# A fused hybrid decoder layer on one core: the beginning reordered, the turned x kept through DRAM, bias rows copied per head pair, GpSimd ordered by hand

## The chip, the cores and the metric

The kernel runs on one core of one Trainium2 chip. The metric is the device time of one execution in microseconds (us). The kernel before takes 1002.67 us, the median of 3 runs (1002.58 to 1002.92).

## What is computed

One step of one decoder layer in float32, for a prompt of 512 tokens and, beside it, 8 samples of 4 tokens (32 more), D = 1024:

```python
def _layer(x, ...):                       # cut to what matters
    h = _rmsnorm(x, norm_mix_pre)
    xr, q, k, v, g = split(h @ w_in)      # 1024 -> 4608 columns
    lru_out = _rg_lru(_causal_dwconv(xr)) # gates, then a scan over time
    attn = _band_attention(q, k, v)       # window 128, 8 query heads on 2 kv heads, table of relative biases
    m = (sigmoid(g_lru) * (lru_out @ w_lru_o) + sigmoid(g_attn) * (attn @ w_attn_o)) @ w_out
    x = x + _rmsnorm(m, norm_mix_post)
    u = _causal_dwconv(_rmsnorm(x, norm_ffn_pre) @ w_up)          # 8192 columns, width 3
    return x + _rmsnorm((gelu(gate(u)) * val(u)) @ w_down, norm_ffn_post)
```

The last rows of the states (LRU, convolutions, keys, values) are outputs too.

## The kernel before

**Products.** Activations stand transposed in SBUF: 128 features on the partitions, 544 tokens in a row, 8 such tiles for D. Every float32 operand is split into a high and a low part of the type fp32r, so a product is three matmuls for each tile of 128: high weight by high h (`hH` with `wh`), high weight by low h (`hL`, `wh`), low weight by high h (`hH`, `wl`). A weight column block ("key") is loaded as 512 KB into one of 5 `raw` buffers; ScalarE (ACT) makes `wh` by a copy (L277), VectorE (DVE) makes `wl` by a subtraction (L282), half a key at a time. The tokens go in two halves: a = 0 is the first 256, a = 1 the other 288 (272 and 272 after the attention).

**Order.** TensorE (PE) is ordered by hand over the whole program, ACT and DVE inside the mixer (everything up to the output of `w_out`); GpSimd (POOL) and the DMA queue of SyncE (SP) are ordered by the framework's scheduler. An engine executes its own instructions in that order. `step` issues one product (24 matmuls) and then calls `tick`, which issues in this order: the `wh` splits of later weights, the side jobs that are due at this tick (generators started by `start_at`), the work on the previous product's result, the `wl` splits, and what the side jobs left in `last`. So a product's result is worked on beside the next product.

**Beginning (L357 to L463).** x0 and x1 (the first 256 tokens) come as two half rows each, are squared and summed by ACT and DVE (`xsquares`), the reciprocal root is made in six small steps (`xrstd`), x is scaled by it (`xscale`, L423 on ACT and L425 on DVE), PE turns 128x128 tiles into PSUM (`ps_ta`, L448), and `hsplit` (L431) makes `hH` on ACT and `hL` on DVE. 18 matmuls on constants keep PE busy before that. Then the first product of the first key is issued in three runs of 8 matmuls. `norm_b` (L451) does the same for the other 288 tokens between the next products (`ps_tb`, L461); its squares stand in the first tick, its root and scaling in the second, its transposes behind the third product.

**Bias table.** `attn_tables` (L544) makes 8 rows of 384 biases by a matmul, stores them in DRAM (`rscr`), and copies each 128 times in DRAM (`rrep`, one DMA of 1024 rows); `load_btab` (L577) loads for each pair of heads a skewed window of it.

**x again (L995 to L1011).** The residual needs x transposed but not normalised. While the products with `w_lru_o` (`pmlo`) run, `x_again` loads x from the inputs once more into `raw` buffers (`xx`), PE transposes it (`pxx`, L1004, 40 transposes), and ACT and DVE copy the pieces into `x1`. Beside each of these products DVE multiplies its result by the gate (L171, `gl`), POOL adds the attention's share (L1019, `gl<-gl,ga`), and ACT and DVE split the sum (`mH`, `mL`) for the product with `w_out`.

**End.** `load` (L1285) brings the weights of the second part of the layer; the last blocks of `w_up` go through `raw` buffers and are combined on DVE, `needs` (L1274) names which of them a sum needs.

## Time and profile before

| what | value |
|---|---|
| median of 3 runs | 1002.67 us |
| the profiled execution | 1003.73 us |
| its span in the trace | 1002.0 us |
| mean granted clock of TensorE | 0.997 |
| busy: PE, DVE, ACT, POOL | 988.9, 732.0, 579.4, 151.0 us |

The profiled execution is 1.73 us longer than its span (what lies ahead of the first and behind the last instruction) and 1.06 us above the median. Rows of the timeline and of the chain begin with the start and the duration in us; a row "x8" joins eight like instructions. In square brackets stands how long the engine was idle ahead of it and what released it.

### The profile page before, as it was taken

How to read it: one execution, taken by the hardware profiler on the slowest of the kernel's cores; microseconds unless marked ns; L12 is line 12 of the kernel's file. 1: busy time of each engine (PE TensorE's matmuls, PEld its weight loads, DVE VectorE, ACT ScalarE, POOL GpSimd, SP SyncE). 2: the span in 40 equal slices, each digit the busy share in tenths (PEclk: the TensorE clock that was granted, in tenths of full speed). 3: DMA queues.
4: the chain of work that ended last, by engine and by line, in shares of the span. 5: the costliest groups of instructions: out<-in, count | busy, mean ns of one | idle time of the engine just before them, and what ended most of it. 6: DMA issues, size and time to landing. Idle time of an engine off the chain costs nothing.

```text
span 1002.0 us, 20195 instructions
## 1 busy us (share of the span) xinstructions
PE 988.9 (99%) x7837; PEld 978.5 (98%) x7837; DVE 732.0 (73%) x1555; ACT 579.4 (58%) x1422; POOL 151.0 (15%) x270
## 2 busy tenths in 40 slices
PE   8999999999999999999999999999999999999997
PEld 7999999999999999999999999999999999999996
DVE  6476687545846555589777788888888888887865
ACT  6444455469358535456776756565656565656652
POOL 3131010002304432110001111111111111110004
PEclk9999999999999999999999999999999999999999
DMA  7743223333322345327245858586867676767712
GB/s 211 231 150 93 64 77 105 99 91 94 102 68 85 106 138 148 105 66 210 71 116 124 193 124 192 125 191 127 189 133 184 139 177 145 171 160 167 216 45 90
DMA packets 207687, 133.40 MB, mean 133 GB/s; under 512 B 6546, under 2 KB 194306, under 8 KB 207560
## 3 DMA queue, kind: packets, MB, share of 16 engines
q1 hardware_dynamic: 197944, 112.20, 39.4%
q0 software_dynamic: 9600, 17.90, 11.3%
q10 hardware_dynamic: 48, 2.03, 0.5%
q8 instruction: 61, 1.00, 0.4%
q14 instruction: 34, 0.28, 0.1%
HBM read 111.82 MB, written 9.14 MB: 121 GB/s over the span
## 4 chain that ended last, share of the span: by engine, by line
PE 92%; DVE 3%; ACT 2%; DMA 2%; issue 0%; SPq 0%; ACTq 0%; DVEq 0%
PE pmin L165 22%; PE pmdn L165 16%; PE pux L1400 15%; PE puy L1400 7%; PE pq L1400 6%; PE pmout L165 5%; PE pmao L165 5%; PE pmlo L165 4%; PE puz L1400 4%; PE pg L165 1%; PE psc L165 1%; PE pvp L165 1%; DMA raw_up_s<-in_w_up_dram 1%; DMA raw_in<-in_w_in_dram 1%; PE pt L701 1%; PE ptok L165 1%
## 5 line engine op out<-in xcount | busy, mean ns | idle before, releaser
L165 PE MATMUL pmin<-hH,wh_in 128*128 128x256 f32 (+1 forms) x576 | 167.8, 294 | 0.0
L165 PE MATMUL pmin<-hH,wl_in 128*128 128x256 f32 (+1 forms) x576 | 164.7, 288 | 0.0
L165 PE MATMUL pmin<-hL,wh_in 128*128 128x256 f32 (+1 forms) x576 | 164.6, 288 | 0.0
L165 PE MATMUL pmdn<-fH,wh_dn 128*128 128x256 f32 (+1 forms) x448 | 129.2, 288 | 0.2 <-DVE ft L174 0.2
L165 PE MATMUL pmdn<-fH,wl_dn 128*128 128x256 f32 (+1 forms) x448 | 129.2, 288 | 0.2 <-DVE wl_dn L168 0.2
L165 PE MATMUL pmdn<-fL,wh_dn 128*128 128x256 f32 (+1 forms) x448 | 129.1, 288 | 0.0
L177 DVE SCALAR_TENSOR_TENSOR uc<-u,fv,uc 128x560 f32<-128x560 f32 x128 | 102.0, 797 | 13.3 <-ACT uc L1431 13.2
L165 PEld LDWEIGHTS pmin<-hH,wh_in 128*128 128x128 f32 x576 | 108.9, 190 | 1.9 <-issue 1.2
L165 PEld LDWEIGHTS pmin<-hL,wh_in 128*128 128x128 f32 x576 | 108.1, 188 | 0.0
L165 PEld LDWEIGHTS pmin<-hH,wl_in 128*128 128x128 f32 x576 | 107.9, 188 | 0.0
L165 PEld LDWEIGHTS pmdn<-fH,wh_dn 128*128 128x128 f32 x448 | 84.5, 189 | 0.6 <-issue 0.6
L165 PEld LDWEIGHTS pmdn<-fH,wl_dn 128*128 128x128 f32 x448 | 84.4, 188 | 0.4 <-DVE wl_dn L168 0.4
L165 PEld LDWEIGHTS pmdn<-fL,wh_dn 128*128 128x128 f32 x448 | 84.3, 188 | 0.0
L1526 ACT COPY u<-pux 128x272 f32<-128x272 f32 x52 | 20.1, 387 | 86.1 <-PE pux L1400 86.1
L168 DVE TENSOR_TENSOR u<-puy,u 128x240 f32<-128x240 f32 (+2 forms) x78 | 24.6, 344 | 49.8 <-PE puy L1400 32.1
L174 DVE TENSOR_TENSOR ft<-ft,pmdn 128x256 f32<-128x256 f32 (+1 forms) x104 | 45.2, 436 | 16.7 <-PE pmdn L165 16.1
L277 ACT ACTIVATE wh_in<-raw_in 128x512 fp32r<-128x512 f32 x72 | 44.2, 629 | 19.3 <-PE pmin L165 8.4
L282 DVE TENSOR_TENSOR wl_in<-raw_in,wh_in 128x512 fp32r<-128x512 f32 x72 | 48.2, 683 | 0.8 <-ACT wh_in L277 0.8
L1431 ACT ACTIVATE uc<-u,fv 128x560 f32<-128x560 f32 x64 | 48.2, 754 | 0.0
L664 ACT ACTIVATE s<-s,st 128x256 f32<-128x256 f32 (+1 forms) x32 | 15.2, 475 | 50.4 <-DVE st L661 43.0
L168 DVE TENSOR_TENSOR wl_dn<-raw_dn,wh_dn 128x512 fp32r<-128x512 f32 x56 | 38.3, 684 | 0.0
L1326 POOL DMA_DIRECT2D raw_up_s<-raw_up_s x26 | 22.7, 874 | 102.9 <-issue 5.2
(776 smaller groups left out, 3404.3 us busy)
## 6 DMA issues: line engine op xcount, KB each, us to landing
raw_in<-in_w_in_dram SPq DMA_DIRECT2D x36, 512.0 KB
raw_dn<-in_w_down_dram SPq DMA_DIRECT2D x56, 256.0 KB
raw_up_s<-in_w_up_dram SPq DMA_DIRECT2D x26, 512.0 KB
raw_up_s<-raw_up_s POOLq DMA_DIRECT2D x26, 256.0 KB, 5.9
raw_ao<-in_w_attn_o_dram SPq DMA_DIRECT2D x8, 512.0 KB
raw_lo<-in_w_lru_o_dram SPq DMA_DIRECT2D x8, 512.0 KB
raw_out<-in_w_out_dram SPq DMA_DIRECT2D x8, 512.0 KB
x1d<-x SPq DMA_DIRECT2D x8, 272.0 KB
```

The source lines that it names most:

```text
L165: pe.matmul(out, l, r, start=start, stop=stop)
L168: dve.tensor_tensor(out=out, in0=a, in1=b, op=ALU.subtract)
L174: dve.tensor_tensor(out=out, in0=a, in1=b, op=ALU.add)
L177: dve.scalar_tensor_tensor(out=out, in0=a, scalar=s_, in1=b, op0=op0, op1=op1)
L277: act.activation(hl[0], raw, AF.Copy)
L282: (eng or dve).tensor_tensor(out=hl[1], in0=raw, in1=f32(hl[0]), op=ALU.subtract)
L664: act.activation(s3[:, j, :], s3[:, j, :], AF.Exp, bias=ng[:, j:j + 1], accum_out=sm[:, j:j + 1])
L701: pe.transpose(pt[:, (2 * ch + j) * P:(2 * ch + j + 1) * P], s3[:, j, ch * P:(ch + 1) * P], ident)
L1326: pool.dma_start(out=w["p4"], in_=w["p2"], accum_op=ALU.add)
L1400: pe.matmul(ps[:, :HN], w, x, start=start and k == 0 and i == 0, stop=stop and k == 3 and i == 2, skip_group_check=True)
L1431: act.activation(yt[j][:, 0:FLATU], u[:, 0:FLATU], AF.Copy, scale=fv[:, j:j + 1])
L1526: act.copy(e[nm_], z)
```

## The change

It has five parts.

1. **Beginning.** The load of the norm's weight rows goes ahead of x1 on SP; four more small loads go from POOL's queue to SP, ahead of the loads of keys 3 and 4. 12 warm matmuls stand ahead of the transpose of these rows and 11 behind it. The scaling of x0 and x1 is three halves on DVE, one on ACT, ahead of the first split of weights. The 16 transposes go into four whole PSUM banks, 8 at a time, and the splits take tiles from alternating banks. The matmuls of the first product (`first_ps`) stand between the splits: `hH` by `wh` and, one tile behind, `hL` by `wh`; the eight `hH` by `wl` come last. The `wl` of the first key is made by POOL instead of DVE. The copy of the weight rows goes from DVE to ACT.
2. **x again.** The turned, scaled x (still without the norm's weight) is copied from PSUM to SBUF: 8 copies of 128x256 and 8 of 128x288, half on ACT and half on DVE, in the first ticks (`keep_a`, `keep_b`). POOL stores the eight tiles to DRAM at ticks 13 to 20, SP stores the reciprocal of the scale. In the stage of `w_lru_o`, SP loads both back and POOL multiplies, 8 times 128x544 (L1048 of the changed kernel). The second load of x, its 40 transposes and 40 copies are gone.
3. **Bias rows.** `rrep` is four tensors of 256 rows, each written by a DMA of its own shortly before it is read.
4. **POOL by hand.** Its order inside the mixer is the program's; loads for the sample tables go from POOL's to SP's queue.
5. **End.** The last block of `w_up` comes in two halves into `s` slots (53 instead of 52) and earlier, not into a `raw` buffer.

```diff
-S_BUFS = 52
+S_BUFS = 53
...
 SAMPLE = (41, 46)
-WARM = 18
+WARM = 12
+KEEP = 11
...
     cp = mixer.enter_context(tc.tile_pool(name="mixer_const", bufs=1))
-    mixer.enter_context(tc.manual_schedule(engines={act.engine, dve.engine}))
+    mixer.enter_context(tc.manual_schedule(engines={act.engine, dve.engine, pool.engine}))
...
         n = X.half[a][1] - X.half[a][0]
-        if key == order[0] and a == 0:
-            for j, (i0, i1) in enumerate(((0, 0), (1, 0), (0, 1))):
-                for k in ks:
-                    mm(ps[:, :n], wunits[2 * wpos[key] + k // 4][i0][:, k % 4, :], X.get(k, a, i1),
-                       j == 0 and k == 0, j == 2 and k == KD - 1)
-            return
...
-        ps = PM("pm" + "_".join(str(z) for z in key) + f"_{a}")
-        if quick:
+        first_ = key == order[0] and a == 0
+        ps = first_ps if first_ else PM("pm" + "_".join(str(z) for z in key) + f"_{a}")
+        if first_:
+            pass
+        elif quick:
...
     xload(0)
+    nc.sync.dma_start(out=rows_a[0:8, :], in_=I["norm_mix_pre"].rearrange("o (k p) -> (o k) p", p=P))
     xload(1)
-    nc.sync.dma_start(out=rows_a[0:8, :], in_=I["norm_mix_pre"].rearrange("o (k p) -> (o k) p", p=P))
...
     xload(4)
-    for i in (2, 3, 4):
-        wload(i)
+    wload(2)
...
     pool.memset(relx, 1.0)
-    pool.dma_start(out=relx[0:NBK, :], in_=I["rel_bias"])
+    nc.sync.dma_start(out=relx[0:NBK, :], in_=I["rel_bias"])
     ohp = T("ohp")[:NBK + 1, 0:3 * WIN]
-    pool.dma_start(out=ohp, in_=I["c_ohp"])
+    nc.sync.dma_start(out=ohp, in_=I["c_ohp"])
     for r, nme in ((8, "norm_mix_post"), (16, "norm_ffn_pre"), (24, "norm_ffn_post")):
-        pool.dma_start(out=rows_a[r:r + 8, :], in_=I[nme].rearrange("o (k p) -> (o k) p", p=P))
+        nc.sync.dma_start(out=rows_a[r:r + 8, :], in_=I[nme].rearrange("o (k p) -> (o k) p", p=P))
+    wload(3)
+    wload(4)
...
     pe.transpose(ps0[:, 0:8], rows_a[0:8, :], ident[0:8, 0:8])
+    for z in range(KEEP):
+        mm(pw[:, (z % 4) * P:(z % 4 + 1) * P], ones, ident, True, True)
...
     xsquares(1)
+    act.copy(pv[:, 0:8], ps0[:, 0:8])
     xrstd(0, 2)
-    split = [wsplit_hi(u) for u in wclaim(2)]
-    xscale(0, "av")
-    xscale(1, "vv")
-    dve.tensor_copy(pv[:, 0:8], ps0[:, 0:8])
-    for u in split:
-        wsplit_lo(*u)
+    u0, u1 = wclaim(2)
+    def scale0(i, z):
+        dve.tensor_scalar(xt[i, z][:, 0:512], xt[i, z][:, 0:512], ss[:, 1, i:i + 1], None, ALU.mult)
+    scale0(0, 0)
+    scale0(1, 0)
+    act.activation(xt[1, 1][:, 0:512], xt[1, 1][:, 0:512], AF.Copy, scale=ss[:, 1, 1:2])
+    scale0(0, 1)
+    first_ps = PM("pm_first")
+    def first_mm(k, i0, i1, start=False, stop=False):
+        mm(first_ps[:, :256], wunits[k // 4][i0][:, k % 4, :], h.get(k, 0, i1), start, stop)
+    ps_ta = []
+    wsplit_lo(*wsplit_hi(u0), eng=pool)
+    seq = (0, 2, 1, 3, 4, 6, 5, 7)
+    for z, k in enumerate(seq + (None,) * 3):
+        if z % 4 == 0 and z < KD:
+            for kk in (z // 2, z // 2 + 1):
+                ps_ta.append(PX(f"ps_ta{kk}"))
+                for q in range(4):
+                    pe.transpose(ps_ta[-1][:, q * P:(q + 1) * P], xtile(q % 2, 2 * kk + q // 2), ident)
+        if k is not None:
+            hsplit(k, 0, ps_ta[k // 2][:, k % 2 * 256:k % 2 * 256 + 256])
+        if z == 1:
+            wsplit_lo(*wsplit_hi(u1), eng=pool)
+        if 2 <= z < KD + 2:
+            first_mm(seq[z - 2], 0, 0, start=z == 2)
+        if z >= 3:
+            first_mm(seq[z - 3], 0, 1)
     for k in range(KD):
-        ps = (PM if k in (5, 6) else PX)(f"ps_ta{k}")
-        for i in range(2):
-            pe.transpose(ps[:, i * P:(i + 1) * P], xtile(i, k), ident)
-        hsplit(k, 0, ps[:, :256])
+        first_mm(k, 1, 0, stop=k == KD - 1)
+    xn = [S(f"xn{k}") for k in range(KD)]
+    xdram = drp.tile([KD, P, NT], F32, name="xdram")
+    rms = cp.tile([P, 5], F32, name="rms")
+    rmsd = drp.tile([5, P], F32, name="rmsd")
+    def keep_a(k):
+        (dve.tensor_copy if k % 2 else act.copy)(xn[k][:, 0:256], ps_ta[k // 2][:, k % 2 * 256:k % 2 * 256 + 256])
+    def keep_b(k, ps):
+        (act.copy if k % 2 else dve.tensor_copy)(xn[k][:, 256:NT], ps[:, :288])
+    def put_away():
+        dve.reciprocal(rms, ss[:, 1, :])
+        nc.sync.dma_start(out=rmsd.rearrange("i p -> p i"), in_=rms)
+        for k in range(KD):
+            pool.dma_start(out=xdram[k], in_=xn[k][:, 0:NT])
+            yield
...
         last.extend(lambda i=i: xsquares(i) for i in (2, 3, 4))
-        yield
+        last.extend(lambda k=k: keep_a(k) for k in range(4))
+        yield
+        last.extend(lambda k=k: keep_a(k) for k in range(4, KD))
...
                 pe.transpose(ps[:, t0 - 256:t0 - 256 + n], xtile(i, k), ident[:n, :n])
-            late.append(lambda k=k, ps=ps: hsplit(k, 1, ps[:, :288]))
+            late.append(lambda k=k, ps=ps: (hsplit(k, 1, ps[:, :288]), keep_b(k, ps)))
...
     for t in range(DT):
-        pool.dma_start(out=rel4[32 * t:32 * t + 32, :], in_=I["rel_bias"])
+        nc.sync.dma_start(out=rel4[32 * t:32 * t + 32, :], in_=I["rel_bias"])
...
     rscr = drp.tile([NH, 3 * WIN], F32, name="rscr")
-    rrep = drp.tile([NH, P, 3 * WIN], F32, name="rrep")
+    rrep = [drp.tile([2, P, 3 * WIN], F32, name=f"rrep{hp}") for hp in range(4)]
...
-        a = rscr[:, :]
-        pool.dma_start(out=rrep, in_=bass.AP(a.tensor, a.offset, [[3 * WIN, NH], [0, P], [1, 3 * WIN]]))
...
         ohs = T("ohs")[:, 0:SKEY]
-        pool.dma_start(out=ohs, in_=I["c_ohs"])
+        nc.sync.dma_start(out=ohs, in_=I["c_ohs"])
...
             m_ = T(f"mk{g}")[:, 0:SKEY]
-            pool.dma_start(out=m_, in_=I["c_msk"][g])
+            nc.sync.dma_start(out=m_, in_=I["c_msk"][g])
...
+    def load_rep(hp):
+        r = rscr[2 * hp:2 * hp + 2, :]
+        pool.dma_start(out=rrep[hp], in_=bass.AP(r.tensor, r.offset, [[3 * WIN, 2], [0, P], [1, 3 * WIN]]))
...
         bt = S(f"btab{hp}")[:, 0:512].rearrange("p (h j) -> p h j", h=2)
-        src = rrep[2 * hp:2 * hp + 2, :, :]
+        src = rrep[hp][:, :, :]
...
     start_at(1, norm_b())
+    start_at(13, put_away())
...
     for hp in range(4):
-        start_at((5, 11, 18, 27)[hp], once(load_btab, hp))
+        start_at((4, 6, 13, 20)[hp], once(load_rep, hp))
+        start_at((5, 10, 17, 26)[hp], once(load_btab, hp))
...
-    def x_again(i):
-        t0, n, src = TOK[i]
-        x_i = RAW(f"xx{i}")
-        nc.sync.dma_start(out=x_i[:n, :], in_=src)
-        yield 2 + i // 4
-        for kk in range(2):
-            px = PX(f"pxx{i}_{kk}")
-            for j in range(4):
-                k = 4 * kk + j
-                pe.transpose(px[:, j * P:j * P + n], x_i[:n, k * P:(k + 1) * P], ident[:n, :n])
+    def x_again():
+        full = T("rms_full")[:, 0:NT]
+        a = rmsd[:, :]
+        nc.sync.dma_start(out=full, in_=bass.AP(a.tensor, a.offset, [[0, P], [1, NT]]))
+        for k in range(KD):
+            nc.sync.dma_start(out=x1[k][:, 0:NT], in_=xdram[k])
+        yield 3
+        for k in range(KD):
+            pool.tensor_tensor(out=x1[k][:, 0:NT], in0=x1[k][:, 0:NT], in1=full, op=ALU.mult)
             yield
-            for j in range(4):
-                k = 4 * kk + j
-                (dve.tensor_copy if j % 2 else act.copy)(x1[k][:, t0:t0 + n], px[:, j * P:j * P + n])
-    for i in range(5):
-        start_at(now[0] + 3 + 2 * i, x_again(i))
+    start_at(now[0] + 3, x_again())
...
         _, p_, nm = key
+        if p_ == 31 and nm == "a12":
+            return [("up", p_, ""), ("up", 32 + p_, ""), ("up", p_, "s")]
...
             src = w_dn[q * CH * P:(q + 1) * CH * P, c * P:(c + 1) * P]
+        elif key == ("up", 31, "s"):
+            raws[key] = [S(f"{nm}{z}")[:, 0:512].rearrange("p (k n) -> p k n", k=4) for z in range(2)]
+            for z, raw in enumerate(raws[key]):
+                nc.sync.dma_start(out=raw, in_=w_up[512 * z:512 * z + 512, 31 * P:32 * P].rearrange("(k p) n -> p k n", p=P))
+            return
...
         r = raws["up", 32 + p_ if nm in ("p1", "a22") else p_, "s" if nm in ("p2", "p4") else ""]
+        if isinstance(r, list):
+            return r[nm == "p4"]
```

Two places of the order matter for what follows. First VectorE in the beginning, from the split of the second key (`raw_in_111`) to the root for the other 288 tokens (the rows on `ss` that end with 128x3); `jv` are the squares, `kL` the work on the first product's result. Before:

```order
L282 TENSOR_TENSOR wl_in_318<-raw_in_111,wh_in_317 128x512
L282 TENSOR_TENSOR wl_in_321<-raw_in_111,wh_in_320 128x512
L409 SCALAR_TENSOR_TENSOR jv_326,ss<-x_1_115 128x512
L409 SCALAR_TENSOR_TENSOR jv_330,ss<-x_1_119 128x512
L409 SCALAR_TENSOR_TENSOR jv_334,ss<-x_1_123 32x512
L168 TENSOR_TENSOR kL_371<-pmin_0_292,kH_370 128x256
L282 TENSOR_TENSOR wl_in_363<-raw_in_125,wh_in_362 128x512
L282 TENSOR_TENSOR wl_in_366<-raw_in_125,wh_in_365 128x512
L174 TENSOR_TENSOR ss<-ss 128x3
```

The same place in the changed kernel:

```order
L408 SCALAR_TENSOR_TENSOR jv_349,ss<-x_1_123 32x512
L479 COPY xn_274<-ps_ta_209 128x256
L479 COPY xn_276<-ps_ta_214 128x256
L169 TENSOR_TENSOR kL_390<-pm_first,kH_389 128x256
L283 TENSOR_TENSOR wl_in_382<-raw_in_125,wh_in_381 128x512
L283 TENSOR_TENSOR wl_in_385<-raw_in_125,wh_in_384 128x512
L479 COPY xn_278<-ps_ta_234 128x256
L479 COPY xn_280<-ps_ta_239 128x256
L175 TENSOR_TENSOR ss<-ss 128x3
```

Four copies of the kept x now stand ahead of the root, two of them ahead of `kL` and of the split of the third key; ACT has four as well, two ahead of its split of the third key and two ahead of its square root.

Second GpSimd in the stage of `w_lru_o`; `gl` are the additions behind the products, the four DMAs store outputs of the recurrent branch. Before:

```order
L1019 TENSOR_TENSOR gl_4158<-gl_4158,ga_2728 128x272 x2
L1019 TENSOR_TENSOR gl_4247<-gl_4247,ga_2826 128x272 x2
L907 DMA out_dram<-lru_rows 3x1024
L908 DMA out_dram<-lru_rows 24x1024
L909 DMA out_dram<-lru_rows 16x1x64
L910 DMA out_dram<-lru_rows 8x1024
L1019 TENSOR_TENSOR gl_4325<-gl_4325,ga_2922 128x272 x2
```

The same place in the changed kernel, where `x_0` to `x_7` are the eight tiles of x:

```order
L1048 TENSOR_TENSOR x_3_4618<-x_3_4618,rms_full 128x544
L1059 TENSOR_TENSOR gl_4291<-gl_4291,ga_2870 128x272
L950 DMA out_dram<-lru_rows 3x1024
L951 DMA out_dram<-lru_rows 24x1024
L952 DMA out_dram<-lru_rows 16x1x64
L953 DMA out_dram<-lru_rows 8x1024
L1048 TENSOR_TENSOR x_4_4619<-x_4_4619,rms_full 128x544
L1059 TENSOR_TENSOR gl_4369<-gl_4369,ga_2966 128x272
```

A multiplication of 128x544 now stands ahead of eight of the sixteen additions, one of them behind the four DMAs as well.

## The prediction

> **What bounds the kernel now.** I read the page first: the busy times and the chain that ended last.
>
> ```profile
> PE 988.9 (99%) x7837; PEld 978.5 (98%) x7837; DVE 732.0 (73%) x1555; ACT 579.4 (58%) x1422; POOL 151.0 (15%) x270
> PE 92%; DVE 3%; ACT 2%; DMA 2%; issue 0%; SPq 0%; ACTq 0%; DVEq 0%
> ```
>
> TensorE (PE) is busy for 988.9 of 1002.0 us, and 92% of the chain is its work. So the time falls only where PE has less to do or waits less, and it rises where another engine makes PE wait. The sum of all PE idle time is 13.1 us, an upper bound for anything that only removes waits. Next I read PE's waits:
>
> ```profile
> PE ps_ta L448 <- ACT x L423: 3.4, 1, 3.4
> PE ps_warm L165 <- POOL relx L374: 1.5, 1, 1.5
> PE pxx L1004 <- DMA xx<-in_x_prompt_dram: 0.9, 1, 0.9
> ```
>
> Three waits make up nearly half of it. Two lie in the beginning, one is at the second load of x, which the change removes.
>
> **x kept through DRAM: PE loses its transposes.** The chain through the stage of `w_lru_o` shows them one group of four at a time, and the tile's own view gives the count:
>
> ```profile
> 350.67 0.44 PE pxx L1004 x4
> 368.50 4.50 DMA xx<-in_x_prompt_dram
> 373.00 0.14 issue
> 373.14 0.63 PE pxx L1004 x4
> 377.21 6.03 PE pmlo L165 x48
> 386.82 0.36 PE pxx L1004 x4
> L1004 PE MATMUL pxx<-ident,xx x40: 221/272/299, 350.5 to 387.0; 128*128 128x128 f32 x32, 32*128 32x32 f32 x8
> ```
>
> Forty transposes in ten groups: seven of 0.44 us, one of 0.63 (behind the wait), two of 0.36 for the 32 samples, in all 3.08 + 0.63 + 0.72 = 4.43 us. The products around them take 3.0 us each (6.03 for two, 24 matmuls of 0.125 us apiece) and follow without a gap, so PE's time falls by all of this. Ahead of the seventh group PE idles for 0.9 us on the load and 0.14 us on its issue, 1.0 us. This wait goes with its transposes. What is late next? The load waited for a `raw` buffer; the new loads go into `s` slots, and nothing on PE reads them here. Term: **-5.4 us**.
>
> **What is added beside it.** POOL gets eight multiplications of 128x544. The rows before have none of this shape; nearest are its two-input operations of 128x568, and DVE's scan beside one of them and without one:
>
> ```profile
> 317.94 1.76 POOL L881 TENSOR_TENSOR xc<-xc,lt 128x568 f32<-128x568 f32 x1
> 319.91 1.40 POOL L881 TENSOR_TENSOR xc<-xc,lt 128x568 f32<-128x568 f32 x1
> 326.74 1.95 POOL L881 TENSOR_TENSOR xc<-xc,lt 128x568 f32<-128x568 f32 x1 [0.68 <-ACT lt L880]
> 320.00 2.50 DVE L887 TENSOR_TENSOR_SCAN hs<-rg,xc 128x568 f32<-128x568 f32 x1 [1.58 <-POOL xc L884]
> 323.97 1.33 DVE L887 TENSOR_TENSOR_SCAN hs<-rg,xc 128x568 f32<-128x568 f32 x1
> L1019 POOL TENSOR_TENSOR gl<-gl,ga 128x272 f32<-128x272 f32 x15 | 16.3, 1087 | 35.9 <-DVE gl L171 26.1 <-ACT wh_lo L277 6.3 <-ACT wh_out L277 3.5
> 368.46 0.78 POOL L1019 TENSOR_TENSOR gl<-gl,ga 128x272 f32<-128x272 f32 x1
> 375.76 0.68 DVE L282 TENSOR_TENSOR wl_lo<-raw_lo,wh_lo 128x512 fp32r<-128x512 f32 x1
> 350.50:364.90 14.40, 14.40 (x120) 14.32 (x119) 8.49 (x21) 5.76 (x16) 3.91 (x4) 1.00 0.35 110
> ```
>
> I take 1.4 to 1.95 us for a multiplication and 1.09 for an addition, 2.5 to 3.04 a product, against the 3.0 that a product lasts: POOL, idle for 35.9 us at these additions now, becomes just about full. Behind a late addition stand ACT's `mH`, then DVE's `mL`, then the next gate multiplication and the next `wl` split, in that order. The cover is what PE has in hand: the last `wl` of the stage is done at 376.44, and its product is the second of the two that begin at 377.21; its second half, which reads this split, is reached at 377.21 + 3.02 + 1.5 = 381.7, 5.3 us later. Once the four output DMAs, which end where the addition at 368.46 begins, push POOL back by some 2 us, and a multiplication stands behind them; 2 us plus eight times 0.04 stay inside 5.3. DVE has room: 8.49 of 14.4 us, and its own copies of x go (as ACT's do). I cost this at nothing; without the cover it is the slower rival below.
>
> The Trainium skill says in "SBUF — State Buffer", section "SBUF: two separate sides", that VectorE operations with two SBUF inputs and a GpSimd operation exclude each other, the later one standing still for the whole of the other; this speaks against the change. The scan of 2.50 us agrees: 1.17 us longer than its twin, beside 1.31 us of a POOL operation. By that rule DVE could lose up to eight times 1.95 us here, and the sum would still stand while the loss stays inside the cover.
>
> **The beginning.** I put PE, ACT and DVE side by side:
>
> ```profile
> 11.07 2.90 PE L448 MATMUL ps_ta<-ident,x 128*128 128x128 f32 x16 [3.43 <-ACT x L423]
> 16.37 1.11 PE L165 MATMUL pmin<-hL,wh_in 128*128 128x256 f32 x8
> 17.32 0.28 PE L165 MATMUL pmin<-hH,wh_in 128*128 128x256 f32 x1
> 20.25 0.81 PE L165 MATMUL ps_ohp<-ohp,relx 33*8 33x384 f32 x2
> 23.92 2.19 PE L461 MATMUL ps_tb<-ident,x 128*128 128x128 f32 x12
> 9.26 1.15 ACT L277 ACTIVATE wh_in<-raw_in 128x512 fp32r<-128x512 f32 x2 [0.69 <-DMA raw_in<-in_w_in_dram]
> 10.31 0.71 ACT L423 ACTIVATE x<-x,ss 128x512 f32<-128x512 f32 x1
> 11.55 3.03 ACT L433 ACTIVATE hH<-ps_ta,pv 128x256 fp32r<-128x256 f32 x8 [0.53 <-PE ps_ta L448]
> 18.34 0.36 ACT L599 ACTIVATE kH<-pmin 128x256 fp32r<-128x256 f32 x1
> 21.66 1.34 ACT L423 ACTIVATE x<-x,ss 128x512 f32<-128x512 f32 x2 [0.83 <-DVE ss L177]
> 12.05 3.23 DVE L177 SCALAR_TENSOR_TENSOR hL<-ps_ta,pv,hH 128x256 fp32r<-128x256 f32 x8
> 18.73 0.42 DVE L168 TENSOR_TENSOR kL<-pmin,kH 128x256 fp32r<-128x256 f32 x1 [0.43 <-ACT kH L599]
> 20.27 0.16 DVE L174 TENSOR_TENSOR ss<-ss 128x3 f32<-128x3 f32 x1
> 21.66 1.67 DVE L425 TENSOR_SCALAR x<-x,ss 128x512 f32<-128x512 f32 x4
> ```
>
> Now: scaling ends at 11.02, the first `hH` starts at 11.55, the last `hL` ends at 15.28, and the two last runs of the first product go on to 17.32. In the change the scaling on ACT stands ahead of the weights (0.71 us from 9.39, since the root is ready when DVE starts its scaling), one split of 0.57 follows, and the first transposes need only the first half of the rows: `hH` can start at about 10.75. Its eight take 3.03 again, with the second split of weights between them: the last `hL` ends near 14.9. By then two of the three runs are done, and only eight matmuls remain (1.11 us, as the run at 16.37). The second product starts at about 16.0, not 17.32: PE is **1.3 us ahead**.
>
> Does it keep that? It needs x2 to x4 scaled for `ps_tb`. PE reaches these transposes after two products and the bias matmul, 23.92 - 17.32 = 6.6 us after its start: at 22.6, or about 23.0, since the split of the third key is later too (below). Now the first three halves that it needs are ready at 23.0: ACT's two end at 21.66 + 1.34, DVE's third at about the same time. So 0.9 us of slack stand before 23.92. The change puts four copies of 128x256 on each engine ahead of the root. Nearest rows: 0.36 for `kH`, 0.42 for `kL`, and 0.38 to 0.40 apiece in the rows of eight (3.03/8, 3.23/8); four are 1.4 to 1.6 us. Off this go 0.3 us, as `hL` ends earlier, and what DVE idles now ahead of `kL` (0.43) is mostly lost again, since ACT's `kH` is also two copies later. The root moves from 20.27 to about 21.5, the scaled halves from 23.0 to about 24.25, and `ps_tb` starts there instead of at 23.92. Term: **+0.3 us**, bounded by -0.9 (PE finds x ready at 23.0) and +1.2 (copies at 0.42 each on both engines, and the small loads put ahead of keys 3 and 4 delay a weight by some tenths). PE's lead of 1.3 us is then spent waiting. The 11 added matmuls lie in the 3.43 us wait and cost nothing.
>
> **The end.** The last block of `w_up` is on the chain, and PE waits there a little:
>
> ```profile
> 917.04 7.29 DMA raw_up_s<-in_w_up_dram
> 928.31 0.28 PE L165 MATMUL pmdn<-fL,wh_dn 128*128 128x256 f32 x1
> 928.76 0.38 PE L165 MATMUL pmdn<-fH,wl_dn 128*128 128x256 f32 x1 [0.17 <-DVE wl_dn L168]
> 929.93 0.28 PE L165 MATMUL pmdn<-fH,wl_dn 128*128 128x256 f32 x1
> 930.26 0.39 PE L1400 MATMUL pux<-b22H,wh_s_p 128*128 128x272 f32 x1
> ```
>
> The load is issued when a `raw` buffer comes free, and lands at 924.33; in the change it needs no such buffer. PE's matmuls at 928.76 and 930.26 start 0.45 and 0.33 us after the one before, where 0.125 us is the spacing in a row: 0.32 and 0.2 us are lost. Term: **-0.5 us**, between 0 and -1.4 (if the later waits for DVE and ACT in the last 50 us shrink as well).
>
> **Bias rows, POOL's order, stores of x.** The four smaller copies of bias rows and the eight stores move the same or 2.2 MB more over hundreds of us in which PE does not wait; the memset that moves into POOL's chain ahead of a scan is 0.1 us apiece. I take 0, bounds -0.3 and +1.
>
> **Sum.** -5.4 + 0.3 - 0.5 = -5.6 us. The profiled execution took 1003.73 (1.06 above the median), so 998.1 in its terms; against the median of 1002.67, **997.1 us**.
>
> **Rivals.**
>
> *The beginning keeps its lead.* If copies from PSUM to SBUF overlap waits better than I assume, `ps_tb` starts at 23.0: -5.4 - 0.9 - 0.5 = -6.8, 995.9 us. For it speaks that DVE and ACT idle 0.4 and 1.8 us in this stretch; against it that the idle time lies behind the dependence, not ahead. 0.20.
>
> *POOL's split of the first key is late.* Two operations of 128x512 at 1.3 to 1.8 us, beside DVE's `hL`. If DVE blocks POOL until 15.3, the `wl` is done only at 18, the second product starts there and `ps_tb` at 24.6 to 25: -5.4 + 0.9 - 0.5 = -5.0, 997.7; with a stall behind it, 998.5. 0.15.
>
> *Half of the transposes' gain comes back.* PE is 5.4 us earlier at the product with `w_out`, and its weights, whose loads stand behind those of x1 in SP's queue, are not ready: about -2.9, 999.8 us. 0.09. Against it: the second load of x moved the same bytes in the same place.
>
> *POOL becomes the bound (slower).* If lock or load makes a pair of multiplication and addition last longer than 3.0 us, the loss is 8 x (pair - 3.0) + 2 - 5.3 us. It eats all 5.6 us from a pair of 4.1 us, that is a multiplication of 3.0. Twice the 1.76 us row gives a pair of 4.6 and a loss of 9.5: 1006.6 us. For it: 2.50 against 1.33 us shows that the two engines hinder each other. Against: no POOL row here is above 1.95. 0.06.
>
> **How the numbers follow.** My forecast has 0.50, the rivals 0.20, 0.15, 0.09 and 0.06. Differences under 0.2% (2.0 us) count as no change, about what a measurement of this kernel can tell. The range reaches from the lead kept together with most of the end's bound (994.8) to half of the gain lost (1000.4). Forecast and first two rivals are faster; half of the third and a little of the fourth fall within 0.2%: faster 0.85, same 0.09, slower 0.06.
>
> **What would show it.** Right: no `pxx`, products of 3.0 us in a row through the stage, `ps_tb` within 1 us of 23.9 with PE idle ahead of it, released by the scaling of x. Wrong: PE waits for `wl_lo`, `wl_out` or a gate's product beside POOL multiplications above 3 us; a second product later than 17.3; a new wait behind an output or bias table in POOL's queue between 30 and 150 us.

## The result and the profile after

The changed kernel takes 1001.03 us, the median of 22 executions (999.40 to 1004.66), against 1002.71 us for 22 of the kernel before. The ratio is 0.9983 with a 95% interval of [0.9975, 0.9991]: faster by 1.7 us, a third of the 5.6 us forecast and outside the range. By the forecast's own measure, under 2.0 us, this counts as no change, to which it gave 0.09. The profiled execution took 1000.44 us, span 998.6 us, so by the two profiled executions 3.3 us are gained. The gap between 3.3 and 1.7 is spread: the profiled execution of before was 1.02 us above the median of these 22, that of the change 0.59 us below its own. First the busy times on the page of the changed kernel, then PE's waits in it:

```profile
PE 986.9 (99%) x7807; PEld 975.4 (98%) x7807; DVE 733.4 (73%) x1541; ACT 578.1 (58%) x1411; POOL 166.9 (17%) x279
```
```profile
PE ps_warm L166 <- POOL relx L369: 1.5, 1, 1.5
PE pkn L779 <- POOL vn L694: 1.2, 1, 1.2
PE ps_tb L503 <- ACT x L422: 0.7, 2, 0.4
PE pmin L166 <- DVE wl_in L283: 0.4, 1, 0.4
```

The 0.9 us wait for the second load of x is gone. The 3.4 us wait for the scaling is in part filled and not gained, since the 11 added matmuls run in it: it is 0.2 us here, up to 1.4 in other traces with these matmuls, and 2.0 without them (experiment 4). Three waits are new: for POOL's copy `vn`, for the scaling of x2 to x4, and for a weight's low part. To see what each costs I compared the start of the same instruction of PE in both traces:

| from | to | before, us | change, us | difference |
|---|---|---|---|---|
| start | `ps_tb` | 23.92 | 24.36 | +0.44 |
| `ps_tb` | first attention product (`psc`) | 19.72 | 20.86 | +1.14 |
| `psc` | sample attention (`pss`) | 131.10 | 132.35 | +1.25 |
| `pss` | first product with `w_lru_o` | 160.76 | 160.46 | -0.30 |
| that | first product with `w_out` | 54.73 | 49.11 | -5.62 |
| that | last product with `w_up` | 558.14 | 557.60 | -0.54 |
| that | end of the span | 53.57 | 53.87 | +0.30 |

So 6.5 us were gained and 3.1 us lost, nearly all the loss within the first 180 us.

**The stage of `w_lru_o`** is what was forecast. Its chain is PE alone:

```profile
338.19 24.10 PE pmlo L166 x192
362.29 0.44 PE plr L947 x4
362.72 3.03 PE pmlo L166 x24
365.76 0.44 PE plr L947 x4
366.19 21.10 PE pmlo L166 x168
```

Beside it, POOL and DVE in this stage:

```profile
351.90 1.36 POOL L1048 TENSOR_TENSOR x<-x,rms_full 128x544 f32<-128x544 f32 x1
354.05 1.09 POOL L1059 TENSOR_TENSOR gl<-gl,ga 128x272 f32<-128x272 f32 x1 [0.79 <-DVE gl L172]
369.34 1.38 POOL L1048 TENSOR_TENSOR x<-x,rms_full 128x544 f32<-128x544 f32 x1
370.67 0.77 POOL L1059 TENSOR_TENSOR gl<-gl,ga 128x272 f32<-128x272 f32 x1
```
```profile
L169 DVE TENSOR_TENSOR mL<-gl,mH 128x272 fp32r<-128x272 f32 x14 | 10.2, 730 | 17.4 <-ACT mH L1062 17.4
```

The same row of the kernel before:

```profile
L168 DVE TENSOR_TENSOR mL<-gl,mH 128x272 fp32r<-128x272 f32 x14 | 6.2, 443 | 6.0 <-ACT mH L1022 5.5
```

A multiplication takes 1.36 us, less than the 1.4 to 1.95 I took. It does hold DVE up: `mL` has a mean of 730 ns against 443 in the kernel before, and 442 in experiment 7, which leaves the multiplications out. Six of the 14 `mL` run beside a multiplication of x and take 1.10 to 1.13 us; the other eight take 0.42 to 0.44. The Trainium skill's rule in "SBUF — State Buffer", section "SBUF: two separate sides", fits this: VectorE and GpSimd operations that need the shared port wait for each other. PE does not notice: from 338 to 387 us it has no wait in this trace.

**The wait at `pkn`.** The chain shows it, and POOL's timeline what led to it:

```profile
90.74 0.12 PE pkn L778
90.94 0.48 POOL btab L624
91.67 0.38 POOL vn L694
92.09 0.30 PE pkn L779
```
```profile
68.19 1.17 POOL L618 DMA_DIRECT2D rrep<-rscr  x1
69.35 2.17 POOL L488 DMA_DIRECT2D xdram<-xn  x4
90.94 0.74 POOL L624 DMA_DIRECT2D btab<-rrep  x1 [19.41 <-PE pkn L778]
91.67 0.37 POOL L694 COPY vn<-v 128x32 f32<-128x32 f32 x1
```

POOL issues the third copy of bias rows at 68.19, four stores of the kept x right behind it, and then the load `btab`, which waits for that copy to land. The copy lands at 90.38, 21.0 us after the end of its issue, and the load is issued at 90.94; the two copies before landed after 13.1 and 10.8 us. Behind it in POOL's order stands `vn`, a copy of 0.37 us that PE's transpose needs. (The row names PE as releaser, since `pkn` was the last thing done before. It is the landing: in experiment 3, too, the load is issued 0.56 us behind the landing, at 90.01, and `pkn` had been at 89.05.) In the kernel before the one copy had landed long before, and `vn` ran 13 us behind the load:

```profile
66.48 0.79 POOL L581 DMA_DIRECT2D btab<-rrep  x1
79.88 0.21 POOL L651 COPY vn<-v 128x32 f32<-128x32 f32 x1 [12.61 <-ACT v L649]
```

**The beginning.** PE, ACT and DVE of the changed kernel:

```profile
24.36 0.33 PE L503 MATMUL ps_tb<-ident,x 128*128 128x128 f32 x1 [0.42 <-ACT x L422]
24.97 2.13 PE L503 MATMUL ps_tb<-ident,x 128*128 128x128 f32 x11 [0.28 <-ACT x L422]
32.99 0.38 PE L166 MATMUL pmin<-hH,wl_in 128*128 128x256 f32 x1 [0.40 <-DVE wl_in L283]
```
```profile
23.58 1.34 ACT L422 ACTIVATE x<-x,ss 128x512 f32<-128x512 f32 x2 [0.83 <-DVE ss L178]
29.02 0.40 ACT L482 COPY xn<-ps_tb 128x288 f32<-128x288 f32 x1 [0.98 <-DVE hL L178]
```
```profile
21.54 0.75 DVE L479 COPY xn<-ps_ta 128x256 f32<-128x256 f32 x2
22.20 0.16 DVE L175 TENSOR_TENSOR ss<-ss 128x3 f32<-128x3 f32 x1
32.26 1.28 DVE L283 TENSOR_TENSOR wl_in<-raw_in,wh_in 128x512 fp32r<-128x512 f32 x2
```

The root moved from 20.27 to 22.20, and `ps_tb` starts when ACT has scaled its first half row of x, at 24.36. Only the first of the twelve transposes can run on it; the second, and with it the rest, waits for ACT's second half row and begins at 24.97, so the product behind them starts at 27.03, where it was at 26.04 before. Then the copies of 128x288 stand between the splits: ACT waits 0.98 us ahead of each of its own until DVE has read the same bank, and the `wl` split that was at 27.80 now starts at 32.26. PE waits for it. Its row in the kernel before:

```profile
27.80 1.28 DVE L282 TENSOR_TENSOR wl_in<-raw_in,wh_in 128x512 fp32r<-128x512 f32 x2
```

### The profile page after: what moved, and what is told of

It is laid out like the page before. It is cut to its first block, busy times and chain, and to the rows that moved or that the text cites. A ratio compares the mean times of both kernels' runs of the same rounds, so it can differ in the third digit from the quotient of the medians.

```text
span 998.6 us, 20168 instructions
## 1 busy us (share of the span) xinstructions
PE 986.9 (99%) x7807; PEld 975.4 (98%) x7807; DVE 733.4 (73%) x1541; ACT 578.1 (58%) x1411; POOL 166.9 (17%) x279
## 4 chain that ended last, share of the span: by engine, by line
PE 92%; DVE 3%; ACT 3%; DMA 1%; issue 0%; SPq 0%; POOL 0%; ACTq 0%; DVEq 0%
PE pmin L166 21%; PE pmdn L166 17%; PE pux L1449 16%; PE puy L1449 8%; PE pq L1449 6%; PE pmout L166 5%; PE pmlo L166 5%; PE pmao L166 5%; PE puz L1449 4%; PE pg L166 1%; PE psc L166 1%; PE pvp L166 1%; PE pt L744 1%; PE ptok L166 1%; DMA x<-in_x_prompt_dram 1%; ACT wh_in L278 0%
```

## The experiments

Experiments 1 to 4, 5 to 8 and 9 to 11 were measured in three groups, each on one chip and with executions of the kernel before beside it, whose medians were 1003.02, 1003.22 and 1002.95 us (1002.71 beside the changed kernel). Medians within a group are compared directly; across groups they carry this difference of up to 0.5 us.

**1. The bias load behind `vn`.**

```diff
-        start_at((5, 10, 17, 26)[hp], once(load_btab, hp))
+        start_at((5, 10, 19, 26)[hp], once(load_btab, hp))
```

> Theory A: the changed kernel lost 1.2 us at 90.6 us, and a varying amount in other executions, because POOL's copy of the samples' values (vn) stands behind the third bias load, which waits for its copy of bias rows to land. With that load moved from tick 17 to 19, behind vn, PE does not wait at the transposes of kn and vn; the profile is about 1.2 us shorter than the changed kernel's (1000.4 to about 999.2), the median falls by more, from 1001.0 to about 999.3, and the spread of over 4 us between executions shrinks to about 1. Theory B: the spread comes from the TensorE clock in the first 20 us, which differs from execution to execution; then only the 1.2 us go (median about 999.8) and the spread stays at 4 us.

Measured: 999.71 us, 6 executions from 998.51 to 1001.94; ratio to before 0.9968 [0.9956, 0.9980]. POOL's timeline of this kernel:

```profile
82.96 0.21 POOL L694 COPY vn<-v 128x32 f32<-128x32 f32 x1 [11.40 <-ACT v L692]
93.00 0.74 POOL L624 DMA_DIRECT2D btab<-rrep  x1 [5.39 <-DMA rrep<-rscr]
```

`vn` is made when v is there, the wait of PE is gone, and the copy of bias rows still lands only at 92.44. The cause of the wait is thus the order on POOL, together with a late landing. The spread shrank only from 5.3 us (22 executions) to 3.4 (6), so theory A explains the wait and not all of the spread. Its profiled execution (1000.62 us) shows two other things that vary: x1 came 0.5 us later than in the changed kernel's trace, and the clock was half in one window:

```profile
23.76:27.17 3.41, 2.71 (x17) 1.00 0.20 54
27.17:30.58 3.41, 3.41 (x16) 0.50 0.39 103
```

The same stretch of the changed kernel's own trace, cut at the windows of its clock, and of experiment 3:

```profile
21.36:24.77 3.41, 2.90 (x23) 1.00 0.18 52
24.77:28.18 3.41, 3.21 (x20) 1.00 0.08 10
```
```profile
20.97:24.38 3.41, 2.71 (x21) 1.00 0.20 52
24.38:27.79 3.41, 3.41 (x24) 1.00 0.10 15
```

Columns: stretch, length, PE's busy time with its instructions, granted clock, DMA share and rate. The wait at `ps_tb` is the same 0.7 us in all three. In the changed kernel it is divided over two windows. In experiments 1 and 3 it falls into one, with PE busy for the same 2.71 us, and yet only the first of them is followed by half the clock; the last section looks at what differs. The half window costs 0.8 us: from `ps_tb` to `psc` 21.67 instead of 20.86.

**2. The copy of bias rows early.**

```diff
-        start_at((4, 6, 13, 20)[hp], once(load_rep, hp))
+        start_at((4, 6, 9, 20)[hp], once(load_rep, hp))
```

> The third copy of bias rows is issued at tick 9 instead of 13, ahead of the stores of the kept x; the order of vn behind the bias load stays. If the landing is late because the copy shares the DMA engines with the stores behind it and other loads (theory A in full), it lands well before 90 us, the wait at kn and vn goes, and times are as with the later load (about 999.3). If the wait has another cause in POOL's queue, the 1.2 us stay and the median stays at 1001.

Measured: 998.53 us, 5 executions from 997.98 to 1000.14; ratio 0.9960 [0.9947, 0.9973]. The POOL timeline of this kernel:

```profile
43.14 1.06 POOL L618 DMA_DIRECT2D rrep<-rscr  x1
70.56 0.73 POOL L624 DMA_DIRECT2D btab<-rrep  x1
84.12 0.21 POOL L694 COPY vn<-v 128x32 f32<-128x32 f32 x1 [12.84 <-ACT v L692]
```

With the order of `btab` and `vn` as in the change, the load no longer waits, nor does PE. My forecast of 997.1 is 1.5 us below this median, against 3.9 below the changed kernel's. How much of the 2.5 us between them is this wait isn't settled: experiment 1 takes the same wait away and lies 1.2 us higher, with 6 executions against 5 and overlapping intervals. The profiled execution is also lucky in the arrival of x1 (the sum of squares of its last half row is read at 6.96 us, against 8.24 in the changed kernel's trace).

**3. The copies of 128x288 at the end of their tick.**

```diff
-            late.append(lambda k=k, ps=ps: (hsplit(k, 1, ps[:, :288]), keep_b(k, ps)))
+            late.append(lambda k=k, ps=ps: (hsplit(k, 1, ps[:, :288]), last.append(lambda: keep_b(k, ps))))
```

> The eight copies of 128x288 go from between the splits to the end of their tick, behind the split of weights. Theory: they and their waits between ACT and DVE delay a weight's low part, for which PE waits 0.55 us at 32.3 us, so this wait goes: the offset against the kernel before at the first attention product falls from +1.6 to about +1.0 us; the profile is 0.5 to 0.6 us shorter, the median by as much (1000.5), the spread unchanged. Rival: the weight's split is late for another reason (its ACT half, or the load), nothing changes by more than 0.1 us at that place.

Measured: 1000.98 us, 12 executions from 998.52 to 1003.13. The wait for `wl_in` is gone, and from `ps_tb` to `psc` PE takes 20.20 instead of 20.86 us, as expected. The median is only 0.05 us below the changed kernel's of another group; taken against the kernel before of each group the gain is 0.4 us. In this trace the wait at `pkn` is longer, 1.7 us instead of 1.2: PE comes to it 1.53 us earlier than in the changed kernel (its first transpose starts at 89.05, against 90.58), but the copy of bias rows lands only 0.93 us earlier (89.45 against 90.38). A wait that ends with a landing takes back part of what was won ahead of it.

**4. Warm matmuls as before (18 and 0).**

```diff
-WARM = 12
-KEEP = 11
+WARM = 18
+KEEP = 0
```

> The warm matmuls as in the kernel before: 18 ahead, none behind the transpose of the weight rows. Theory A: in this stretch the clock is half for one window of 3.4 us, which costs the opening at most 0.3 us, since the scaling of x sets the start of the transposes at 24.4 us; the spread between executions stays over 4 us. Theory B: the 11 matmuls and the clock in the beginning make the spread: without them it falls to that of the kernel before (most executions within 0.5 us), at a median 1 to 2 us different.

Measured: 1002.75 us, 11 executions from 1001.17 to 1004.48, ratio 0.9997 [0.9989, 1.0006]. Against expectation the median is 1.7 us above the changed kernel's, 1.4 against the kernel before of each group. Its profiled execution is 1.75 us longer too, and the trace says where: it has the longest wait at `pkn` of all (2.0 us, 0.8 more) and half the clock from 27.20 to 30.61 (0.86 us more from `ps_tb` to `psc`). The stretch behind the place of the 11 matmuls takes as long as in the change (12.52 us from the first product to `ps_tb`, 12.51 there), and a half window at the same place stands in experiments 1 and 8, which have these matmuls. But the clocks of all executions speak for them: without them 7 of 11 have a mean granted clock of 0.995 or 0.996, in experiments 1 to 3 of the same group 4 of 23. That the matmuls hold up the clock is thus likely, not shown. The spread is 3.3 us: not over 4 as in theory A, and not half a microsecond as in theory B.

**5. Experiments 2 and 3 together.** The two edits above.

> The third copy of bias rows at tick 9 and the copies of 128x288 at the end of their tick. Theory: two separate losses, 1.2 us or more at 90 us and 0.55 us at 32 us; both waits are gone, the median is 0.5 us below the kernel with the early copy alone (998.5), about 998.0, and from the start of ps_tb to the first attention product PE takes 0.6 us less than in the changed kernel (20.2 instead of 20.9 us). Rival: the second wait reappears at a later product; no difference to the early copy alone.

Measured: 998.35 us, 6 executions from 997.17 to 1001.41; ratio 0.9958 [0.9945, 0.9970]. From `ps_tb` to `psc` 20.19 us, and no wait at `pkn`. Both waits are gone, but of the 0.5 us expected in the median only 0.2 are seen against experiment 2, within the noise of 5 and 6 executions.

**6. As 5, and four copies of 128x256 behind the root.**

```diff
-        last.extend(lambda k=k: keep_a(k) for k in range(4, KD))
         last.append(lambda: xrstd(2, 5))
         last.extend(lambda i=i, e=e: xscale(i, e) for i, e in ((2, "av"), (3, "av"), (4, "vv")))
+        last.extend(lambda k=k: keep_a(k) for k in range(4, KD))
```

> As before, and four of the eight copies of 128x256 go behind the root and the scaling of x2 to x4 in their tick. Theory (the prediction's term for the beginning): each engine has two copies of 0.33 us less ahead of the root, so from the start of the first product to the start of ps_tb PE takes 0.7 us less (11.9 instead of 12.5 us), and PE waits less there; median about 997.4. Rival: the transposes then wait for the banks that these copies read, and nothing or less than 0.2 us is gained.

Measured: 997.94 us, 5 executions from 996.84 to 998.37; ratio 0.9945 [0.9932, 0.9958]. This is the lowest median here, clearly below the kernel before and the change; from experiment 5 it can't be told apart (the intervals overlap). From the first product to `ps_tb` PE takes 11.93 instead of 12.51 us, near the expected 11.9; 0.35 us of it is given back behind (20.54 from `ps_tb` to `psc`, against 20.19). PE's wait for the scaled x at `ps_tb` shrinks from 0.7 to 0.26 us:

```profile
23.45 0.27 PE L503 MATMUL ps_tb<-ident,x 128*128 128x128 f32 x1
23.98 2.13 PE L503 MATMUL ps_tb<-ident,x 128*128 128x128 f32 x11 [0.26 <-ACT x L422]
```

Two new waits of PE stand in this kernel's trace: 0.3 us for `qL`, and one like the rival's, for a copy out of a bank, though it is a copy of 128x288:

```profile
PE ps_tb L503 <- DVE xn L482: 0.4, 1, 0.4
```

All five executions show a mean clock of 0.999; in experiment 5 three of six were at 0.996 to 0.998. This fits the reading that a short wait there no longer costs a window; with so few executions it isn't proven.

**7. The second load of x, with the early copy of bias rows.** `x_again` as in the kernel before; the stores are made but not read.

```diff
-    def x_again():
-        full = T("rms_full")[:, 0:NT]
...
-            pool.tensor_tensor(out=x1[k][:, 0:NT], in0=x1[k][:, 0:NT], in1=full, op=ALU.mult)
-            yield
-    start_at(now[0] + 3, x_again())
+    def x_again(i):
+        x_i = RAW(f"xx{i}")
...
+                pe.transpose(px[:, j * P:j * P + n], x_i[:n, k * P:(k + 1) * P], ident[:n, :n])
...
+    for i in range(5):
+        start_at(now[0] + 3 + 2 * i, x_again(i))
```

> The early copy of bias rows, and in the stage of w_lru_o the second load of x with its 40 transposes and 40 copies as in the kernel before (the stores of the kept x stay and are not read). Theory: the stage, from the first product with w_lru_o to the first with w_out, takes 49.1 us in the changed kernel and 54.9 in the kernel before; here again 54.5 to 55, so the median rises by 5.4 to 5.8 us, to about 1004. Rival: POOL's multiplications cost PE something that the trace hides; then the loss is smaller, 4 us or less.

Measured: 1003.72 us, 11 executions; ratio 1.0005 [0.9996, 1.0014]. The stage takes 54.00 us against 48.93 in experiment 2, the medians differ by 5.2 us, 5.0 against the kernel before of each group. The groups of transposes are back, the wait for the load is 0.3 us here instead of 0.9:

```profile
359.48 0.44 PE pxx L1049 x4
359.92 3.02 PE pmlo L166 x24
370.43 3.85 DMA xx<-in_x_prompt_dram
374.42 0.63 PE pxx L1049 x4
```

The main term of the forecast holds. The rest of the change, with this undone but x still kept and stored, gains nothing.

**8. The last block of `w_up` through a `raw` buffer, with the early copy of bias rows.**

```diff
-        if p_ == 31 and nm == "a12":
-            return [("up", p_, ""), ("up", 32 + p_, ""), ("up", p_, "s")]
...
-        elif key == ("up", 31, "s"):
+        elif False:
```

> The early copy of bias rows, and the last block of w_up through a raw buffer as in the kernel before. Theory: PE waits 0.5 to 0.6 us again around 925 us, the median rises by 0.6 us to about 999.1. Rival: the waits come from elsewhere, the median stays at 998.5 within 0.2.

Measured: 1002.58 us, 11 executions; ratio 0.9995 [0.9987, 1.0004]. Not 0.6 but 4 us slower than experiment 2 (3.9 against the kernel before of each group). The chain and PE's wait:

```profile
914.30 8.51 DMA raw_up_s<-in_w_up_dram
```
```profile
PE pux L1447 <- DVE wl_s_p L169: 2.5, 1, 2.5
```

PE is 4.4 us earlier here than in the kernel before, but the load is issued only 2.7 us earlier (914.30 against 917.04) and takes 8.51 instead of 7.29 us: it lands 1.5 us earlier. PE runs into it: from the first statistics after `w_out` to the last product with `w_up` it takes 534.19 us, in experiment 2 530.69. 3.5 of the 5 us won in the mixer are given back at this one place, between 920 and 929 us; behind it 0.5 us come back up to the end of the span.

**9. The beginning without keeping x.** Experiment 7 without `keep_a`, `keep_b`, `put_away` and `xn`.

```diff
-        last.extend(lambda k=k: keep_a(k) for k in range(4))
-        last.extend(lambda k=k: keep_a(k) for k in range(4, KD))
-            late.append(lambda k=k, ps=ps: (hsplit(k, 1, ps[:, :288]), keep_b(k, ps)))
+            late.append(lambda k=k, ps=ps: hsplit(k, 1, ps[:, :288]))
-    start_at(13, put_away())
```

> The changed kernel with the early copy of bias rows, without keeping x: no copies out of PSUM, no stores, and the second load of x in the stage of w_lru_o, as in the kernel before. So of the beginning only its reordering is left. Theory: the copies cost the beginning what its reordering gained. Without them ps_tb starts 11.3 to 11.6 us after the first product instead of 12.5, and the first attention product comes 19.7 us after ps_tb as in the kernel before; measured from the arrival of x1 the beginning is 1.0 to 1.5 us shorter than before, and the median is 1.5 to 2 us below the kernel with copies and second load (1003.7), about 1002. Rival: the beginning is late for another reason (loads moved to SP), then it is not shorter.

Measured: 1001.93 us, 11 executions; ratio 0.9987 [0.9978, 0.9995]. From `ps_tb` to `psc` 19.76 us, as in the kernel before. From the first product to `ps_tb` 12.44 us, not 11.3 to 11.6; here the clock was half for one window from 12.9 us on. Such a window costs 0.8 us in this stretch (experiment 7 has one and takes 13.31 us, the changed kernel 12.51), and 11.6 would be left. But the kernel before has a half window too, from 11.93 on, so the two traces compare like with like: from the reading of x1's squares to the second product 9.45 us here and 9.43 before, to `ps_tb` 16.06 and 16.03. In this trace the reordering gains nothing, as the rival had it. The median came out near the expected 1002 all the same; the early last block, which alone gives 1.3 us (experiment 11), is enough for it. Keeping x costs 1.5 us in the medians (0.50 us above the kernel before in experiment 7, 1.02 below it here) and 2.0 us in the traces, which both have a half window: 0.87 up to `ps_tb`, 1.08 from there to `psc`.

**10. POOL by the framework's scheduler.**

```diff
-    mixer.enter_context(tc.manual_schedule(engines={act.engine, dve.engine, pool.engine}))
+    mixer.enter_context(tc.manual_schedule(engines={act.engine, dve.engine}))
```

> The changed kernel with GpSimd ordered by the framework's scheduler, as before. It puts the third copy of bias rows ahead of most stores, but several multiplications of x ahead of the first additions in the stage of w_lru_o, where they must wait for the loads of x. Theory: PE's wait at kn and vn (1.2 to 2.0 us in the changed kernel) goes or shrinks below 0.5 us, since the copy lands earlier; a late multiplication instead delays the first additions, hidden by the 5.3 us that PE has in hand, or not: median between 999.5 and 1003. Rival: the scheduler's order does not wait anywhere, median 999.0 or less.

Measured: 1004.43 us, 11 executions, ratio 1.0013 [1.0005, 1.0022]; above the upper end of what I expected. The wait at `pkn` is gone, but others take its place:

```profile
342.62 6.65 POOL L1048 TENSOR_TENSOR x<-x,rms_full 128x544 f32<-128x544 f32 x5 [4.55 <-DMA x<-xdram]
349.23 0.77 POOL L1059 TENSOR_TENSOR gl<-gl,ga 128x272 f32<-128x272 f32 x1
```
```profile
PE pmlo L166 <- DVE gl L172: 2.8, 2, 1.4
PE pmin L166 <- DVE qL L169: 1.2, 2, 0.8
```

Five multiplications stand ahead of the first addition and wait for the loads of x; DVE's next gate product comes behind, and PE waits for it. The stage takes 52.33 instead of 49.11 us. This is the mechanism of my slower rival, brought on by order and not by the length of a multiplication.

**11. The early last block alone, in the kernel before.** The edits of part 5 only.

```diff
-S_BUFS = 52
+S_BUFS = 53
...
+        if p_ == 31 and nm == "a12":
+            return [("up", p_, ""), ("up", 32 + p_, ""), ("up", p_, "s")]
...
+        elif key == ("up", 31, "s"):
+            raws[key] = [S(f"{nm}{z}")[:, 0:512].rearrange("p (k n) -> p k n", k=4) for z in range(2)]
...
+        if isinstance(r, list):
+            return r[nm == "p4"]
```

> The kernel before with only the early load of the last block of w_up. Theory: alone this part is worth the 0.5 to 0.7 us that PE waits there, since loads and products arrive there together; it is worth 4 us only in a kernel whose products come 4 to 5 us earlier, because the load does not come earlier with them: median 0.5 us below the kernel before, about 1002.4. Rival: the part is worth 3 to 4 us by itself; median 999 to 1000.

Measured: 1001.61 us, 12 executions; ratio 0.9989 [0.9980, 0.9997]: 1.3 us, more than 0.7 and far from 4. Since experiment 9 has this part too (1001.93), the reordered beginning, with the bias rows and POOL's order, adds nothing to it in the medians.

## Why the prediction was wrong, point by point

- **x again: right.** -5.4 forecast, -5.6 in the traces, 5.2 us in the medians when undone. POOL's multiplications cost PE nothing in the order of the change, and their threat was real (experiment 10).
- **The beginning: the number fits at `ps_tb` by luck, and the term is too small.** +0.3 forecast, +0.44 measured, and the mechanism named, the root behind the copies, is right: experiment 6 takes 0.58 back. But the lead of 1.3 us did not come. The second product starts at 16.99, not at 16.0; x1 came 0.35 us later than in the trace of before, which explains a third. What lead there is goes with the clock, which was half for one window in the trace of before and full here; with a half window in both there is none (experiment 9). The root stands at 22.20, not at 21.5, and ACT's two scaled halves are ready at 24.92, not at 24.25. That `ps_tb` starts near the forecast all the same comes from one transpose that needs only the first of them; the product behind `ps_tb` is 0.99 us late. And the eight copies of 128x288, which stand in the next ticks, were given no term at all; experiment 3 takes 0.66 us back from them. Up to the first attention product the beginning cost 1.58 us, not 0.3.
- **"Bias rows, POOL's order, stores of x. I take 0": the step that failed.** It rested on "over hundreds of us in which PE does not wait". I counted bytes and did not ask, as the prediction itself should have, what is queued behind a waiting instruction on POOL. Behind the third `btab` is `vn`, and PE waits for it: 1.2 us in the profiled execution, up to 2.0 in other traces. Without the wait the median is lower by 1.3 us (experiment 1, 999.71) or 2.5 us (experiment 2, 998.53), and why these two differ stays open. My bound was +1. I named this as a sign of error, without a price.
- **The end: size and reason.** -0.5 forecast, -0.54 in the traces, so it looks right. But what the part is worth depends on the rest: 1.3 us alone, 4 us behind a mixer that is 5 us faster. Without part 5 most of the forecast gain would not have arrived (experiment 8), and the forecast did not see that.
- **Rivals.** The `wl` of the first key is not late: POOL's two splits take 1.3 us each and are done at 14.05, and PE first reads them at 16.05. Nor does PE wait for weights at the product with `w_out`.
- **Range.** Its ends don't follow from their own terms: the lead kept with all of the end's bound gives 995.0, not 994.8, and half of the gain lost gives 999.9, not 1000.4. I took the sum against one execution and carried it over to the median. The executions of the change spread over 5.3 us, and the profiled one lies 0.59 us below their median. The spread goes with the granted clock: of the 22, the 11 with a mean of 0.998 or 0.999 have a median of 1000.02 us, the 11 with 0.995 to 0.997 one of 1002.63. For the 75 executions of the kernel before beside the experiments it is 1002.82 (39 at 0.998 or more) and 1003.25 (36 below). So at the higher clock about 2.8 us are gained, at the lower one 0.6; the forecast had no term for this. Whether the waits bring the lower clock or come with it isn't shown.
- **Open:** how the 1.6 us between the two ways of comparing (3.3 and 1.7) divides among arrival of x1, wait at `pkn` and half windows. The profiled execution of the change had a clock of 0.999, that of before 0.997, which is a part of it. The traces show each of the three vary (squares of x1 read at 7.0 to 8.8 us in kernels with the same loads; 1.2 to 2.0 us; 0 or 0.8 us), not their distribution.

## What to carry to other kernels

For every instruction that waits on a DMA, read the next ones in its engine's queue and price who waits for them, even if they are 0.2 us long; to move either the wait or the short one is often a one-number edit, here worth more than the reordered beginning. A gain in one stage counts only if the loads of later stages come earlier too: look for the place where products and loads arrive together, and test the part that seems small there with the gain in and out. Copies that are "off the path" in a beginning where three engines hand work on in turn belong behind the step that the next stage waits for; here that gave 0.58 us, of which 0.35 came back as other waits.

## What the runs showed of the hardware

The granted clock changed in windows of 3.41 us. PE's busy time in a window does not tell whether the next one is granted half: with 0.7 us of idle PE and 2.70 to 2.71 us busy, the clock of the next window was 0.5 in the traces of experiments 1, 4 and 8, and stayed at 1.00 in those of 3, 7 and 10. What differs is what PE did. Where the clock fell, nearly all of the busy time was transposes, and only 0.32 to 0.69 us other matmuls; where it stayed, these were 1.95 to 2.25 us. The same holds in the kernel before: 2.54 us busy in 5.10 to 8.51, of which 2.37 us were other matmuls, were followed by the full clock, 0.85 us of nothing but transposes in 8.51 to 11.92 by half. In the first 35 us of the 13 traces the clock fell behind windows with at most 0.84 us of other matmuls and stayed behind those with more, with two exceptions (0.81 us in experiment 10 stayed, 1.29 us in experiment 11 fell). Near the end of the program it does not hold: in experiment 5 a window from 986.38 with 0.10 us of other matmuls was followed by the full clock. So this is a reading of the traces that fits the beginning, not a rule, and no run was made to test it. The Trainium skill, "TensorE: Matmul & The Clock Gate", "Part 1: The HAM clock gate", describes windows of this length that run freely beside the kernel; the traces agree with both, and show that a window needn't be idle as a whole for the clock to fall.

The copies of bias rows (384 KB, within DRAM) landed 13.1 and 10.8 us after their issue in the first 60 us of the changed kernel. The third, with four stores of 272 KB issued behind it on the same queue and two copies of 992 KB from another engine's queue begun 3 to 4 us before, took 21.0 us, and the load waiting for it, and all behind that load, paid. The stores alone are slow in this stretch as well: in experiment 2, with no copy of bias rows there, the same four took 14.0 to 14.6 us, while the first store of the changed kernel, at 60.28, took 3.6. How much of the delay comes from each isn't shown.
